# A quarter of the weights' low parts: VectorE subtraction, or negation and accumulating DMA

## The chip, the cores and the metric

The kernel runs on one core of one Trainium2 chip. The time is the device time of one execution in microseconds (us); before the change the runs shown have a median of 2719.02 us. All views of the profile come from one profiled execution.

## The reference

A trunk of two layers over 256 tokens of width 4096. All inputs are float32, and the products must keep nearly that precision.

```python
def reference(x, norm_w, w_in, q_norm, k_norm, ret_decay_fwd, ret_decay_bwd, ret_norm, w_out, final_norm):
    ...
    for l in range(DEPTH):                         # DEPTH = 2
        h = rmsnorm(x, norm_w[l])
        proj = h @ w_in[l]                         # [256, 4096] @ [4096, 11264]
        aq, ak, av, ag, rq, rk, rv, rg = jnp.split(proj, SPLIT_POINTS, axis=-1)
        ...                                        # norms of queries and keys, axial rotation
        a_out = (jax.nn.silu(ag) * gqa_attention(aq, ak, av)).astype(x.dtype)
        ...
        r = bidirectional_retention(rq, rk, rv, log_gf, log_gb).transpose(0, 2, 1, 3)
        r = rmsnorm(r, ret_norm[l]).reshape(B, S, RET_WIDTH)
        r_out = (jax.nn.silu(rg.astype(jnp.float32)) * r).astype(x.dtype)
        x = x + jnp.concatenate([a_out, r_out], axis=-1) @ w_out[l]    # [256, 4096] @ [4096, 4096]
    return rmsnorm(x, final_norm)
```

## The kernel before

Nearly all the work is two large products per layer: 256 tokens against 22 blocks of 512 columns of `w_in` and 8 such blocks of `w_out`, 30 blocks per layer and 60 in all. The contraction of 4096 is cut into 8 chunks of 512 rows. One chunk of one block is 1 MB of weights, the unit of loading: `Weights.load` issues it on SP's queue into one of three buffers `wraw` (L191, L204), after the operand's rows `full` in the first eight chunks.

TensorE multiplies in the format float32r, which keeps fewer bits than float32, so each operand is made of two parts: `hi`, the value cast to float32r, and `lo`, the rest. A product is then three matmuls (`product`, L304 to L308): `hi` with `whi`, `hi` with `wlo`, `lo` with `whi`.

The weights are split in pieces: a chunk has four row blocks of 128 rows, a piece (`WSUB = 2`) has two of them, 128 partitions x 1024 values, 512 KB. `Weights._split` makes a piece's parts: ScalarE copies `wraw` to `whi` with the cast (L219), and VectorE subtracts `whi` from `wraw` into `wlo` (L220). Both tiles have four buffers. A piece serves 2 row blocks x 2 token tiles x 3 = 12 matmuls of 128 x 128 against 512 columns, in `products`. There are 60 x 8 x 2 = 960 pieces; the very first chunk is split row block by row block, so that L219 and L220 have 962 executions.

`block` is the main loop: for each chunk and each of its two pieces the 12 matmuls, then the split of a later piece, then one step of the work beside the stream, and after the chunk the load of a later one. The split is issued under a raised priority (`AHEAD = 200`), and a scheduler orders the instructions of each engine by priority and program order. Each engine works through its own queue in order.

The work beside the stream consists of generators (`tasks`): norms, rotation, gates, transposes by 32 x 32 blocks with copies (`transposed`, L285 and L293), attention and retention with their own small products, and the residual sum. The small products go through the same `product` and stand between the large ones on TensorE.

The operand, 32 row blocks of 256 tokens in two parts, stays on the chip. Between two products of the trunk it is replaced chunk by chunk (`turn_over`): the new chunks wait in DRAM, written from POOL's queue (`put`, L254) and read back on it (`fetch`, L260), and are split by ScalarE and VectorE (`split_operand`, L237 to L244). In layer 0 the residual stream goes to DRAM on the same queue (L633). POOL otherwise computes only powers with the exponent -0.5 for the norms (L177).

At the end, the last two chunks of the last block are computed one token tile at a time, each followed by the final norm and the outputs' stores (`finish`).

Of the kernel before, what the change touches and what calls it, by code (L numbers as in the profile page):

```python
# [11 lines left out]
F32R = mybir.dt.float32r  # L12
AF = mybir.ActivationFunctionType
ALU = mybir.AluOpType
AX = mybir.AxisListType

P = 128
# [9 lines left out]
NB = 512  # L27
KT = D_MODEL // P
KG = 4
NCH = KT // KG  # L30
MT = SEQ // P
WSUB = 2
TMP = 4
ON_DVE = (0,)
# [4 lines left out]

# (kind, index, first column) of the 512-wide column blocks of w_in, in the  # L40
# order in which they are computed.
AQ, AK, AV, AG, RQ, RK, RVO, RG = 0, 2048, 2560, 3072, 5120, 6144, 7168, 9216
# [12 lines left out]

# Columns of the constants' array.
C_COS, C_SIN, C_DP, C_DN, C_END = 0, 256, 512, 1024, 1536


def constants():  # L60
    """Rotary tables and distances between positions: shapes alone."""
    rows = SEQ // GRID_W
    row = np.repeat(np.arange(rows), GRID_W).astype(np.float32)
    col = np.tile(np.arange(GRID_W), rows).astype(np.float32)
    axis = HD // 2
    inv = (10000.0 ** (-np.arange(0, axis, 2, dtype=np.float32) / np.float32(axis))).astype(np.float32)
    ar = (row[:, None] * inv[None, :]).astype(np.float64)
    ac = (col[:, None] * inv[None, :]).astype(np.float64)
    cos = np.concatenate([np.cos(ar), np.cos(ar), np.cos(ac), np.cos(ac)], axis=1)
    sin = np.concatenate([-np.sin(ar), np.sin(ar), -np.sin(ac), np.sin(ac)], axis=1)  # L70
    c = np.zeros((P, C_END), np.float32)
    for m in range(MT):
        c[:, C_COS + HD * m : C_COS + HD * (m + 1)] = cos[P * m : P * (m + 1)]
        c[:, C_SIN + HD * m : C_SIN + HD * (m + 1)] = sin[P * m : P * (m + 1)]
    j = np.arange(P)[:, None, None] + P * np.arange(MT)[None, :, None]
    d = np.arange(SEQ)[None, None, :] - j
    c[:, C_DP:C_DN] = np.maximum(d, 0).reshape(P, -1)
    c[:, C_DN:C_END] = np.maximum(-d, 0).reshape(P, -1)
    return c
# [3 lines left out]
def hybrid_encoder(  # L83
# [15 lines left out]
    nc = tc.nc  # L99
# [15 lines left out]

# [1 line left out]
    cst = t(cp, [P, C_END], "cst")  # L117
# [16 lines left out]
    def log_sigmoid():  # L134
        """lg = min(x, 0) - log1p(exp(-|x|)), log1p(u) = 2 atanh(u / (2 + u)) by its series."""
        n = DEPTH * 2 * RET_HEADS
        u, s, s2, p, a = (t(cp, [P, n], f"ls{i}") for i in range(5))
        nc.scalar.activation(a, dec, AF.Abs)
        nc.scalar.activation(u, a, AF.Exp, scale=-1.0)
        nc.vector.tensor_scalar_add(a, u, 2.0)  # L140
        nc.vector.reciprocal(a, a)
        nc.vector.tensor_mul(s, u, a)
        nc.vector.tensor_mul(s2, s, s)
        nc.vector.tensor_scalar_mul(p, s2, 1.0 / 15.0)
        for d in (13, 11, 9, 7, 5, 3):
            nc.vector.scalar_tensor_tensor(p, p, 1.0 / d, s2, op0=ALU.add, op1=ALU.mult)
        nc.vector.scalar_tensor_tensor(p, p, 1.0, s, op0=ALU.add, op1=ALU.mult)
        nc.vector.tensor_scalar(a, dec, 0.0, 0.5, op0=ALU.min, op1=ALU.mult)
        nc.vector.tensor_sub(p, a, p)
        nc.vector.tensor_scalar_mul(lg, p, 2.0)  # L150

    def halves(v, h):
        """The first or second 32 of each 64 of the last dimension: [P, ..., 2, 32]."""
        return v.rearrange("p (a b e) -> p a b e", b=2, e=HD // 4)[:, :, h, :]

    def rope_tables(kind, l):
        """Tables of cosines and signed sines, with gains and scale folded in."""
        cm = cst[:, C_COS:C_SIN].rearrange("p (m d) -> p m d", m=MT)
        sm = cst[:, C_SIN:C_DP].rearrange("p (m d) -> p m d", m=MT)
        if kind not in ("ak", "aq"):  # L160
            return cm, sm
        c = t(sp, [P, MT, HD], "C")
        s = t(sp, [P, MT, HD], "S")
        g = (kn if kind == "ak" else qn)[:, l * HD : (l + 1) * HD]
        for m in range(MT):
            nc.vector.tensor_mul(c[:, m, :], cm[:, m, :], g)
            for h in range(2):
                nc.vector.tensor_mul(halves(s[:, m, :], h), halves(sm[:, m, :], h), halves(g, 1 - h))
        if kind == "aq":
            nc.vector.tensor_scalar_mul(c, c, HD**-0.5)  # L170
            nc.vector.tensor_scalar_mul(s, s, HD**-0.5)
        return c, s

    def rsqrt(dst, ss, n, count):
        """dst = (ss / count + eps) ** -0.5 on [P, n]."""
        nc.vector.tensor_scalar(dst, ss, 1.0 / count, EPS, op0=ALU.mult, op1=ALU.add)
        nc.gpsimd.tensor_tensor(dst, dst, half[:, :n], op=ALU.pow)  # L177

# [1 line left out]
    class Weights:  # L180
        def __init__(self):
            self.todo = []
            for l in range(DEPTH):
                self.todo += [w_in[l, b, c] for b in range(N_IN) for c in range(NCH)]
                self.todo += [w_out[l, b, c] for b in range(N_OUT) for c in range(NCH)]
            self.loaded = 0
            self.raw, self.parts = [], []

        def load(self):
            if self.loaded < len(self.todo):  # L190
# [8 lines left out]
                for k in range(0, KG, step):  # L199
# [4 lines left out]
                    nc.sync.dma_start(r[:, ks, :], src[:, ks, :])  # L204
                self.raw += [(r[:, i : i + WSUB, :], step) for i in range(0, KG, WSUB)]

# [4 lines left out]
        def _split(self):  # L211
            if self.raw:
                r, step = self.raw.pop(0)
                hi = t(wp, [P, WSUB, NB], "whi", 4, F32R)
                lo = t(wp, [P, WSUB, NB], "wlo", 4, F32R)
                step = min(step, WSUB)
# [5 lines left out]

# [1 line left out]
    full = [None] * NCH  # L224
# [8 lines left out]
    def split_operand(c, gains=None):  # L233
        """hi + lo = full, its rows times gains [P, KG] if given."""
        new_operand(c)
# [14 lines left out]
    def put(c, v):  # L250
        """A finished part of the next operand waits in DRAM; the last ones stay on chip."""
        full[c] = v
# [8 lines left out]

# [1 line left out]
    tasks = []  # L263
# [15 lines left out]
    def transposed(src, room, dst):  # L279
        """dst[:, i, :] = src[:, :, i-th 128].T for i < 4; src and room are [P, MT, 512].  # L280

        Blocks of 32 x 32 are transposed in place in room, and then change places.
        """
        flat = "p m c -> p (m c)"
# [19 lines left out]
    def product(out, a, b, start, stop):  # L304
        """out += a.T @ b for operands in two parts."""
        nc.tensor.matmul(out, a[0], b[0], start=start, stop=False)  # L306
# [22 lines left out]
    def rotary(acc, L, kind, dst):  # L329
        """Queries or keys of four heads: norm, rotation, then [128, 4, 256] transposed."""  # L330
        v = evacuated(acc, L, "tmp", TMP)
# [37 lines left out]
    def gate(acc, L, dst, gain=None):  # L369
        """dst = silu of the block, times gain [P, 512] over both token tiles if given."""  # L370
        e = t(sp, [P, MT, NB], "tmp", TMP)
# [13 lines left out]
    def attention_pair(L, g, h, qT, sgT, mixT):  # L385
        """Heads h and h + 1 of group g."""
        s = [t(ps, [P, MT, SEQ], "ps") for _ in range(2)]
# [55 lines left out]
    def retention_weights(L, i):  # L443
        """(q k) * decay of two heads, [keys, queries]."""
        D = t(sp, [P, MT, 2 * SEQ], "pr", 1).rearrange("p m (a s) -> p (m a) s", a=2)
# [65 lines left out]
    def rstd_of(L, parts, n):  # L511
        """1 / rms of each token from partial sums of squares [P, MT, n]."""
        L.rstd = t(sp, [P, MT], "rstd", 2)
# [64 lines left out]
    def turn_over(c, starts, ends, l=None):  # L578
        """The operand's tiles are replaced as the last block before the change ends.

        l: the layer that begins, if one does.
        """

# [15 lines left out]
    def out_task(l, n, acc):  # L599
        """x plus the block; in the last layer times final_norm, and its sum of squares."""  # L600
        last = l == DEPTH - 1
# [38 lines left out]
    def finish(m):  # L640
        """The last block's columns of one token tile, then that tile's rows of the output."""
        n = N_OUT - 1
# [16 lines left out]

# [1 line left out]
    layers = [Layer() for _ in range(DEPTH)]  # L661
# [27 lines left out]

# [1 line left out]
    for l, L in enumerate(layers):  # L691
# [82 lines left out]
```

## Time and profile before

| What | Before |
|---|---|
| median of the runs | 2719.02 us (2718.59 to 2719.45, 2 runs) |
| profiled execution, first to last instruction | 2716.3 us |
| mean granted TensorE clock | 0.998 |
| TensorE busy | 2697.1 us (99%) |
| VectorE busy | 1768.5 us (65%) |
| ScalarE busy | 1543.6 us (57%) |
| GpSimd (POOL) busy | 55.9 us (2%) |
| DMA | 554.69 MB, mean 204 GB/s |

The profile names engines PE (matmul), PEld (weight load into TensorE), DVE (VectorE), ACT (ScalarE), POOL and SP. A line such as L220 is a line of the kernel, a tile is named by the kernel's own name, and `out<-in` says what an instruction writes and reads. A group's row gives count, busy time, mean duration in ns, and, behind the bar, the idle time of that engine just before these instructions with what ended it. A row of the waits reads: who waited, for whom, total us, times, longest. An engine that idles costs nothing while another sets the end. The matmuls are pipelined: each lasts longer than the distance to the next one.

### The profile page before, as it was taken

What the parts mean: (1) busy time and instruction counts of PE and PEld (TensorE: products, weight loads), DVE (VectorE), ACT (ScalarE), POOL (GpSimd) and SP (SyncE); (2) the same over time, 40 slices, a digit from 0 to 9 for tenths busy, and PEclk for the clock granted to TensorE, in tenths of its full rate; (3) what the DMA queues carried; (4) which work ended last, traced back from release to release, by engine and by line L of the source; (5) the groups of instructions that cost most, each with busy time, mean ns of one, the idle gap of its engine ahead of it and who ended that gap; (6) DMA issues with size and microseconds to landing.
All of it is one profiled execution on the core that took longest, in us unless ns stands there. A gap on an engine that the chain in (4) does not pass through costs nothing.

```text
span 2716.3 us, 31460 instructions
## 1 busy us (share of the span) xinstructions
PE 2697.1 (99%) x12192; PEld 2243.9 (83%) x12192; DVE 1768.5 (65%) x1995; ACT 1543.6 (57%) x2242; POOL 55.9 (2%) x78
## 2 busy tenths in 40 slices
PE   8999999999999999999999999999999999999998
PEld 7888888888888888888888888888888888888886
DVE  6677778766656675545665677787756565755544
ACT  6657667755455555545664576677555455644443
POOL 0000000000000000000000000000000000000000
PEclk9999999999999999999999999999999999999999
DMA  8654554555555565666755545555554555655654
GB/s 313 239 198 170 197 194 179 185 194 198 191 193 186 207 235 207 230 226 249 244 201 190 202 178 186 194 180 185 205 188 182 203 203 194 220 211 211 218 204 178
DMA packets 88454, 554.69 MB, mean 204 GB/s; under 512 B 9840, under 2 KB 10608, under 8 KB 26992
## 3 DMA queue, kind: packets, MB, share of 16 engines
q1 hardware_dynamic: 81968, 529.62, 54.6%
q0 software_dynamic: 6336, 23.07, 2.3%
q8 instruction: 95, 1.56, 0.2%
q14 instruction: 55, 0.45, 0.0%
HBM read 534.82 MB, written 17.83 MB: 203 GB/s over the span
## 4 chain that ended last, share of the span: by engine, by line
PE 99%; DMA 0%; issue 0%; SPq 0%; ACT 0%; DVE 0%; ACTq 0%; POOLq 0%; POOL 0%
PE acc L307 32%; PE acc L308 32%; PE acc L306 32%; PE ps L307 1%; PE ps L306 1%; PE ps L308 1%; DMA wraw<-in_w_in 0%; SPq L203 0%; SPq L204 0%; DVE wlo L220 0%; ACT whi L219 0%; ACT ps L646 0%; ACT kTh L657 0%; DVE full L644 0%; ACTq L770 0%
## 5 line engine op out<-in xcount | busy, mean ns | idle before, releaser
L220 DVE TENSOR_TENSOR wlo<-wraw,whi 128x1024 fp32r<-128x1024 f32 (+1 forms) x962 | 1165.0, 1217 | 821.0 <-ACT whi L219 818.9
L219 ACT CAST whi<-wraw 128x1024 fp32r<-128x1024 f32 (+1 forms) x962 | 1007.3, 1051 | 979.6 <-PE acc L308 945.3
L306 PE MATMUL acc<-whi,hi 128*128 128x512 f32 x3840 | 1496.2, 390 | 7.3 <-ACT whi L219 7.3
L307 PE MATMUL acc<-wlo,hi 128*128 128x512 f32 x3840 | 1495.8, 390 | 0.5 <-DVE wlo L220 0.5
L308 PE MATMUL acc<-whi,lo 128*128 128x512 f32 x3840 | 1495.7, 390 | 0.0
L306 PEld LDWEIGHTS acc<-whi,hi 128*128 128x128 f32 x3840 | 721.7, 188 | 156.0 <-ACT whi L219 7.7
L308 PEld LDWEIGHTS acc<-whi,lo 128*128 128x128 f32 x3840 | 721.5, 188 | 150.6
L307 PEld LDWEIGHTS acc<-wlo,hi 128*128 128x128 f32 x3840 | 721.7, 188 | 149.6 <-DVE wlo L220 1.4
L378 DVE RECIPROCAL tmp<-tmp 128x512 f32<-128x512 f32 x32 | 107.3, 3353 | 1.0
L293 ACT COPY tmp<-tmp 32x256 f32<-32x256 f32 x216 | 87.3, 404 | 18.5 <-DVE tmp L285 15.7
L293 ACT COPY pr<-tmp 32x256 f32<-32x256 f32 x192 | 77.5, 404 | 20.5 <-DVE tmp L285 18.1
L293 ACT COPY full<-tmp 32x256 f32<-32x256 f32 x192 | 77.5, 404 | 9.8 <-DVE tmp L285 7.3
L285 DVE STREAM_TRANSPOSE tmp<-tmp 128x1024 f32<-128x1024 f32 x42 | 52.1, 1242 | 0.9
L293 ACT COPY sg<-tmp 32x256 f32<-32x256 f32 x96 | 38.8, 404 | 12.6 <-DVE tmp L285 11.4
L401 ACT ACTIVATE pr<-ps,st 128x256 f32<-128x256 f32 x64 | 29.8, 475 | 21.2 <-DVE st L397 21.1
L316 ACT ACTIVATE tmp<-acc,rstd 128x512 f32<-128x512 f32 x36 | 24.5, 685 | 26.9 <-PE acc L308 25.6
L243 DVE SCALAR_TENSOR_TENSOR lo<-full,nw,hi 128x256 fp32r<-128x256 f32 x68 | 29.4, 479 | 9.2 <-ACT hi L242 9.2
L242 ACT ACTIVATE hi<-full,nw 128x256 fp32r<-128x256 f32 x68 | 30.1, 500 | 9.1 <-DMA full<-next_dram 3.5
L237 ACT CAST hi<-full 128x1024 fp32r<-128x1024 f32 x18 | 19.0, 1054 | 23.9 <-PE acc L307 15.8
L302 DVE TENSOR_TENSOR pTl<-pr,pTh 128x1024 fp32r<-128x1024 f32 x24 | 29.3, 1220 | 0.0
L373 ACT ACTIVATE tmp<-acc,nrstd 128x512 f32<-128x512 f32 x32 | 22.1, 691 | 10.0 <-PE acc L308 9.9
L396 DVE TENSOR_REDUCE st<-ps 128x2 f32<-128x512 f32 x32 | 21.7, 677 | 8.9 <-PE ps L308 8.9
(146 smaller groups left out, 963.7 us busy)
## 6 DMA issues: line engine op xcount, KB each, us to landing
wraw<-in_w_in SPq DMA_DIRECT2D x351, 1024.0 KB, 4.8
wraw<-in_w_out SPq DMA_DIRECT2D x128, 1024.0 KB, 4.8
next_dram<-full POOLq DMA_DIRECT2D x18, 512.0 KB, 5.1
full<-next_dram POOLq DMA_DIRECT2D x18, 512.0 KB, 4.6
tmp<-in_x SPq DMA_DIRECT2D x16, 512.0 KB, 7.1
x_dram<-tmp POOLq DMA_DIRECT2D x8, 512.0 KB, 3.9
full<-in_xT SPq DMA_DIRECT2D x7, 512.0 KB, 7.5
gain<-in_ret_norm SPq DMA_DIRECT2D x8, 256.0 KB, 3.6
```

Source lines behind the costliest of these rows:

```text
L219: nc.scalar.copy(hi[:, ks, :], r[:, ks, :])
L220: nc.vector.tensor_sub(lo[:, ks, :], r[:, ks, :], f32(hi[:, ks, :]))
L242: nc.scalar.activation(hi[c][:, k, :], full[c][:, k, :], AF.Copy, scale=g)
L243: nc.vector.scalar_tensor_tensor(lo[c][:, k, :], full[c][:, k, :], g, f32(hi[c][:, k, :]), op0=ALU.mult, op1=ALU.subtract)
L285: nc.vector.transpose(room.rearrange(flat), src.rearrange(flat))
L293: copy(to[b, :, :, i, :], fr[a, :, :, j, :])
L302: nc.vector.tensor_sub(parts[1], src, f32(parts[0]))
L306: nc.tensor.matmul(out, a[0], b[0], start=start, stop=False)
L307: nc.tensor.matmul(out, a[0], b[1], start=False, stop=False)
L308: nc.tensor.matmul(out, a[1], b[0], start=False, stop=stop)
L378: nc.vector.reciprocal(e[:, m, :], e[:, m, :])
L401: nc.scalar.activation(pr[:, m, e * SEQ : (e + 1) * SEQ], s[e][:, m, :], AF.Exp, bias=st[:, 0, i : i + 1], accum_out=st[:, 1, i : i + 1],)
```

## The change

From the ninth piece on, every fourth piece (the 12th, 16th, ..., 960th) is made in another way. ScalarE writes the negated cast of the raw weights into `wlo`; a DMA issued from POOL then reads the same weights a second time from DRAM and adds them to `wlo` where it lies, so that it holds the weights less their cast; ScalarE makes `whi` as before. VectorE has no part in such a piece. `whi` and `wlo` get five buffers in place of four, and the scratch space for the descriptors of POOL's DMAs is set to 8192 bytes per partition, where the default is 16384. Comments and docstrings are removed as well; the diff below leaves that out.

```diff
+WBUF = 5
...
     class Weights:
         def __init__(self):
...
             self.loaded = 0
+            self.n = 0
             self.raw, self.parts = [], []
...
-                self.raw += [(r[:, i : i + WSUB, :], step) for i in range(0, KG, WSUB)]
+                self.raw += [(r[:, i : i + WSUB, :], step, src[:, i : i + WSUB, :]) for i in range(0, KG, WSUB)]
...
         def _split(self):
             if self.raw:
-                r, step = self.raw.pop(0)
-                hi = t(wp, [P, WSUB, NB], "whi", 4, F32R)
-                lo = t(wp, [P, WSUB, NB], "wlo", 4, F32R)
+                r, step, src = self.raw.pop(0)
+                hi = t(wp, [P, WSUB, NB], "whi", WBUF, F32R)
+                lo = t(wp, [P, WSUB, NB], "wlo", WBUF, F32R)
+                self.n += 1
+                if self.n > 8 and self.n % 4 == 0:
+                    nc.scalar.activation(lo, r, AF.Copy, scale=-1.0)
+                    nc.gpsimd.dma_start(lo, src, accum_op=ALU.add)
+                    nc.scalar.copy(hi, r)
+                    self.parts.append((hi, lo))
+                    return
                 step = min(step, WSUB)
                 for k in range(0, WSUB, step):
                     ks = slice(k, k + step)
                     nc.scalar.copy(hi[:, ks, :], r[:, ks, :])
                     nc.vector.tensor_sub(lo[:, ks, :], r[:, ks, :], f32(hi[:, ks, :]))
                 self.parts.append((hi, lo))
...
-    nc = bacc.Bacc("TRN2", target_bir_lowering=False, num_devices=1)
+    nc = bacc.Bacc("TRN2", target_bir_lowering=False, num_devices=1, dynamic_dma_scratch_size=8192)
```

## The prediction

> **What bounds the kernel now.** I read the page first (span, busy shares, chain), then the table of stages, then the waits, then the groups and the DMA issues.
>
> ```profile
> span 2716.3 us, 31460 instructions
> PE 2697.1 (99%) x12192; PEld 2243.9 (83%) x12192; DVE 1768.5 (65%) x1995; ACT 1543.6 (57%) x2242; POOL 55.9 (2%) x78
> ...
> PE 99%; DMA 0%; issue 0%; SPq 0%; ACT 0%; DVE 0%; ACTq 0%; POOLq 0%; POOL 0%
> ```
> ```profile
> 1600.00:2000.00 400.00, 400.00 (x1852) 334.52 (x1852) 295.08 (x364) 261.73 (x421) 7.43 (x7) 1.00 0.53 190
> 2600.00:2700.00 100.00, 100.00 (x443) 82.80 (x442) 49.39 (x43) 39.38 (x43) 0.00 (x0) 1.00 0.50 181
> 2700.00:2717.00 17.00, 4.95 (x22) 3.75 (x20) 5.43 (x14) 6.57 (x12) 1.10 (x2) 0.71 0.65 247
> ```
> TensorE is busy in 2697.1 of 2716.3 us and is 99% of the chain that ended last. In the stages shown (columns: length, PE, PEld, DVE, ACT, POOL, clock, DMA share, GB/s) it is busy for the whole stage at a granted clock of 1.00. What it does not use is 2716.3 - 2697.1 = 19.2 us, of which 17.0 - 4.95 = 12.05 us are the last stage, the outputs after the last products. No change of the weights' splitting can win more than 19.2 us, 0.7%. The median of the runs, 2719.0, stands 2.7 us over the span; I carry these 2.7 us along, and make the sum against 2719.0.
>
> ```profile
> ACT whi L219 <- PE acc L308: 945.3, 607, 3.1
> DVE wlo L220 <- ACT whi L219: 818.9, 594, 3.0
> ```
> ```profile
> PE acc L306 <- ACT whi L219: 7.3, 2, 6.0
> PE acc L307 <- DVE wlo L220: 0.5, 1, 0.5
> ```
> The waits (total us, times, longest) point the same way. ScalarE waits for TensorE to give back a buffer of the weights' high part in 607 of 962 cases, VectorE waits behind ScalarE in 594, and TensorE itself waits for weights 7.8 us in all, 6.0 of them for the first piece. The split runs ahead of TensorE and is held back by it. The VectorE subtraction that the change removes is thus hidden already.
>
> **The change part by part.** The stream has 960 pieces of two row blocks (2 layers x 30 blocks x 8 chunks x 2). From piece 12 on, every fourth changes: (960 - 8) / 4 = 238.
>
> ```profile
> L220 DVE TENSOR_TENSOR wlo<-wraw,whi 128x1024 fp32r<-128x1024 f32 (+1 forms) x962 | 1165.0, 1217 | 821.0 <-ACT whi L219 818.9
> L219 ACT CAST whi<-wraw 128x1024 fp32r<-128x1024 f32 (+1 forms) x962 | 1007.3, 1051 | 979.6 <-PE acc L308 945.3
> L242 ACT ACTIVATE hi<-full,nw 128x256 fp32r<-128x256 f32 x68 | 30.1, 500 | 9.1 <-DMA full<-next_dram 3.5
> ```
> *Removed:* 238 subtractions x 1.217 = 290 us of VectorE, 1768 to 1479 us. VectorE is on no part of the chain: worth 0.
>
> *Added on ScalarE:* 238 negations. Their form is not in the trace; the CAST of the same size takes 1.05 us, and four of the scaled copies of a quarter of the size 4 x 0.50 = 2.0. I take the CAST's 1.05 (same size): 250 us, 1544 to 1794 us, 66% of the span; at 2.0 it would be 74%. In the stage 1600 to 2000, with 261.7 of 400 us, 37 us come on top: 75%. The cover is ScalarE's waiting above; gone, it would cost up to these 250 us.
>
> *Added on the DMA queues:* 238 accumulating DMAs of 512 KB, issued from POOL.
>
> ```profile
> q1 hardware_dynamic: 81968, 529.62, 54.6%
> q0 software_dynamic: 6336, 23.07, 2.3%
> ...
> wraw<-in_w_in SPq DMA_DIRECT2D x351, 1024.0 KB, 4.8
> ...
> next_dram<-full POOLq DMA_DIRECT2D x18, 512.0 KB, 5.1
> full<-next_dram POOLq DMA_DIRECT2D x18, 512.0 KB, 4.6
> x_dram<-tmp POOLq DMA_DIRECT2D x8, 512.0 KB, 3.9
> ```
> ```profile
> L260 POOL DMA_DIRECT2D full<-next_dram x18: 527/538/582, 927.2 to 2335.4; - x18
> ...
> DMA to landing us min/median/max: 3.5/4.6/7.2
> ```
> An accumulation into SBUF is not in the trace. The nearest rows are the 44 plain transfers of the same 512 KB on the same queue (18 + 18 + 8): they hold the 16 engines for 2.3% x 2716.3 / 44 = 1.42 us each, and land 4.6 us (loads) or 5.1 us (stores) after issue. Lower end: an accumulation costs what a load costs, 1.42 us of the engines and 4.6 us to landing. Upper end by rows: it reads SBUF as a store does and loads as a load does, one behind the other: 4.6 + 5.1 = 9.7 us. I take twice the engine time, since it reads two operands for one write: 2.84 us, landing 4.6 + 1.42 = 6.0 us.
>
> The Trainium skill (Collectives: The Full Stack, "The bandwidth ceiling: the fold count and why AG ≠ RS ≠ AR") says that an adding DMA is slower than a copying one because it needs two source reads, not because of the add, so that its rate is about half. By that rule the engine time is 2.84 us, as taken; without it the bounds 1.42 and up stand as they are. No row here shows an adding DMA.
>
> *How long the landing may take.* TensorE's pace is the clock:
>
> ```profile
> 1000.11 0.39 PE L306 MATMUL acc<-whi,hi 128*128 128x512 f32 x1
> ...
> 1002.83 0.39 PE L306 MATMUL acc<-whi,hi 128*128 128x512 f32 x1
> ```
> These two starts are 12 matmuls apart, one piece: 2.72 us, 0.227 us per matmul. In the instructions of the built program, five buffers in place of four let a negation start once the piece five places earlier is consumed, and the first matmul that reads the summed low part stands 51 matmuls later in 168 of the 238 cases, 56 to 75 later in 64, 50 in 5, and 33 for the last piece. Fifty matmuls take 11.34 us; less 0.39 - 0.23 = 0.16 for the end of the releasing matmul, 1.05 for the negation and 0.1 for hand-overs, 10.0 us are left for the landing. Against 6.0 that is 4.0 us spare, against 9.7 it is 0.3.
>
> *What eats the spare time.* The longest landing of a plain load is 7.2 - 4.6 = 2.6 us over the median, and ScalarE works in order, so a negation can stand behind other work:
>
> ```profile
> 1144.35 1.05 ACT L219 CAST whi<-wraw 128x1024 fp32r<-128x1024 f32 x1
> 1145.42 2.48 ACT L293 COPY full<-tmp 32x256 f32<-32x256 f32 x6
> 1147.93 1.05 ACT L219 CAST whi<-wraw 128x1024 fp32r<-128x1024 f32 x1
> ```
> A string of six copies holds ScalarE for 2.48 us. Both together: 6.0 + 2.6 + 2.5 = 11.1, 1.1 us too late. ScalarE was busy at the release in (962 - 607) / 962 = 37% of the pieces, and the longest of 18 landings is 1 in 18: 0.37 / 18 x 238 = 5 cases, 5 us at most. I take 2 us. At the upper end (9.7), ScalarE's 37% alone make 88 cases late by about 1 us: 92 us. The last piece has 32 x 0.227 - 1.31 = 5.9 us: 0.1 us late, 3.8 at the upper end; I take 1 us.
>
> *Moved:* on POOL each accumulation stands among the 44 transfers and the small powers of the norms. Nothing that stands ahead of one on POOL depends, in the built order, on a later matmul than its own negation does; behind it wait the powers, which VectorE needs. An issue holds POOL 0.54 us (row above), every 10.9 us. Worth 0, with the rival below if POOL blocks. The smaller descriptor ring, 8192 for the default 16384 bytes, has no row; with one accumulation per 10.9 us and 6.0 to landing hardly more than one is in flight: 0, at the worst a POOL transfer that waits for the one before it.
>
> *Engine time of the DMAs.* Four pieces are 4 x 2.72 = 10.9 us. The two queues above hold the engines 56.9% of it, 6.2 us; with 2.84 it is 9.0 us, 83%. Bytes read grow by 238 x 0.524 = 125 MB, to 250 GB/s on average, and the first slice of the page already moves 313.
>
> ```profile
> GB/s 313 239 198 170 197 194 179 185 194 198 191 193 186 207 235 207 230 226 249 244 201 190 202 178 186 194 180 185 205 188 182 203 203 194 220 211 211 218 204 178
> ```
> *Sum:* 2719.0 + 0 (VectorE) + 0 (ScalarE, hidden) + 2 (late landings) + 1 (last piece) = 2722 us. With the low ends 2719; with the high ends 2719 + 92 + 4 = 2815.
>
> **The rivals.**
> *A, the accumulation overloads the DMA engines* (slower). If it holds them k times as long as a plain load, a group of four pieces needs 6.2 + 1.42 k; above k = 3.3 this is more than 10.9 us and TensorE starves at the rate of the DMAs. At k = 4 it is 11.9 us, 1.0 too long: 238 x 1.0 = 240 us, 2959; each further k adds 338 us. For it: no row shows how an engine does read, add and write, and the engines are over half used. Against it: nothing but the two-reads argument.
> *B, landings at the top of the bounds* (slower): a negation that finds ScalarE busy then stalls TensorE, the 2815 us worked out above. For it: weights' transfers and accumulations share the engines, and the plain loads already spread to 7.2. Against it: 9.7 supposes no overlap of the two reads.
> *C, POOL in order* (slower or within): the 18 fetches wait for a buffer to come free, and an accumulation behind one waits as well.
>
> ```profile
> POOL full L260 <- DVE lo L238: 111.6, 6, 42.3
> ```
> The 42.3 is POOL's idle time since its previous work, not a hold-up by itself. At 1 us for each of POOL's 78 operations it is 78 us, 2797.
> *D, the change does what it says and a gain appears:* at most 19.2 us, 2700, still within 2%.
>
> **How the numbers follow.** The forecast has 0.62 (its own range 2714 to 2750); A 0.22; B 0.10; C 0.05; D 0.01. Some of B and C stays under 2% (2773; 2% is about what a measurement of this kernel can tell from no change): 0.03. So within 2%: 0.62 + 0.03 + 0.01 = 0.66 or so; slower by more: 0.33; faster by more: 0.01, since TensorE's idle time does not allow it. The time is that of the forecast, 2722. The range goes from 2708 (half of the possible gain and a little) to 2960, which takes in B, C and A up to k = 4, and leaves out the heavier half of A, 0.12, and some 0.02 below.
>
> **What would show it.** Right: the new row of the DMA issues lands near 6 us, q0 grows by about 238 x 2.84 / 2716 = 25% to 27%, VectorE falls to about 1480 us and ScalarE rises to about 1794, and TensorE's waits for the accumulation stay under 10 us in all. Wrong: q0 above 45% and weights landing far over 4.8 us (A), landings over 10 us with a wait of TensorE in most groups (B), or waits of accumulations behind other POOL work (C). A negation far from 1.05 us would break ScalarE's term.

## The result and the profile after

The changed kernel takes 2754.48 us (2754.42 to 2754.53, two runs) against 2719.02: 1.0134 times the time before, interval 1.0117 to 1.0152. That is 35 us slower, within the 2% and within the range that the prediction gave, on the side of its forecast but some twelve times as far from the time before as its 2722. The prediction took about 2% for what a measurement of this kernel can tell from no change; the interval shows that a loss of 1.3% is clear.

The page after, rows in the order of the first fences of the prediction:

```profile
span 2752.7 us, 32073 instructions
PE 2710.4 (98%) x12192; PEld 2242.7 (81%) x12192; DVE 1491.3 (54%) x1757; ACT 1765.2 (64%) x2480; POOL 264.1 (10%) x316
...
q1 hardware_dynamic: 81968, 529.62, 51.9%
q0 software_dynamic: 40608, 147.87, 31.0%
...
PE 68%; issue 19%; DMA 8%; DVE 2%; ACT 1%; POOL 1%; SPq 0%; POOLq 0%; ACTq 0%
...
wraw<-in_w_in SPq DMA_DIRECT2D x351, 1024.0 KB, 7.1
wraw<-in_w_out SPq DMA_DIRECT2D x128, 1024.0 KB, 7.2
wlo<-in_w_in POOLq DMA_DIRECT2D x174, 512.0 KB, 8.3
wlo<-in_w_out POOLq DMA_DIRECT2D x64, 512.0 KB, 8.4
```

The span is 36.4 us longer. The chain is no longer TensorE alone: accumulations (the `wlo<-in_w_...` DMAs, 238 of them) hold 7 to 8% of it. ("issue" is time in which an engine waited for nothing that the profile shows.) VectorE has become 277 us lighter, ScalarE 222 us heavier. Loads of weights now take 7.1 us to land where they took 4.8.

The waits after (who waited, for whom, total us, times, longest):

```profile
POOL wlo L221 <- ACT wlo L220: 2012.4, 221, 34.1
DVE wlo L229 <- ACT whi L228: 896.5, 467, 7.1
ACT whi L228 <- PE acc L317: 527.5, 349, 4.4
...
PEld acc L316 <- DMA wlo<-in_w_in: 25.4, 31, 3.3
```
```profile
PE acc L316 <- DMA wlo<-in_w_in: 14.6, 15, 2.9
PE acc L315 <- ACT whi L228: 7.8, 2, 5.8
PE acc L316 <- DMA wlo<-in_w_out: 7.6, 8, 2.2
PE acc L316 <- DVE wlo L229: 0.5, 1, 0.5
```

TensorE has one new wait, 14.6 + 7.6 = 22.2 us for accumulations, in 23 places. That is nearly all of its additional idle time: span less busy is 42.3 us after, 19.2 before, 23.1 more. The other 13 us are busy time: 2710.4 - 2697.1. I added up the distances between the starts of neighbouring matmuls as far as they exceed 227 ns: 8.3 us before (6.3 of them at the start), 44.8 after, 36.5 more, the whole loss. Behind each stall the next matmul starts some 335 in place of 227 ns later, and after the two longest the clock drops. So the loss is stalls of TensorE and what follows directly on each.

One stall, step by step (start, duration, engine):

```profile
1343.45 1.30 ACT L251 ACTIVATE hi<-full,nw 128x256 fp32r<-128x256 f32 x3
...
1344.78 0.40 ACT L302 COPY full<-tmp 32x256 f32<-32x256 f32 x1
1345.21 1.06 ACT L220 ACTIVATE wlo<-wraw 128x1024 fp32r<-128x1024 f32 x1
...
1346.29 0.53 POOL L269 DMA_DIRECT2D full<-next_dram  x1 [8.46 <-DVE lo L252]
1346.81 0.93 POOL L221 DMA_DIRECT2D wlo<-in_w_out  x1
...
1347.23 7.03 SPq L206 DMA_DIRECT2D wraw<-in_w_out  x2
```
```profile
1346.81 10.30 DMA wlo<-in_w_out
1357.11 0.04 issue
1357.16 0.50 PE acc L316
```

ScalarE starts the negation late, behind other work (its buffer had been free for about 1.5 us). POOL first issues a fetch and then the accumulation. 0.4 us later SP issues loads of weights. The accumulation lands 10.3 us after issue, and TensorE starts 0.04 us after that.

### The profile page after: what moved, and what is told of

The parts are those of the page before. It is cut to its first block, busy times and chain, and to the rows that moved or that the text cites. A ratio compares the mean times of both kernels' runs of the same rounds, so it can differ in the third digit from the quotient of the medians.

```text
span 2752.7 us, 32073 instructions
## 1 busy us (share of the span) xinstructions
PE 2710.4 (98%) x12192; PEld 2242.7 (81%) x12192; DVE 1491.3 (54%) x1757; ACT 1765.2 (64%) x2480; POOL 264.1 (10%) x316
## 3 DMA queue, kind: packets, MB, share of 16 engines
q1 hardware_dynamic: 81968, 529.62, 51.9%
## 4 chain that ended last, share of the span: by engine, by line
PE 68%; issue 19%; DMA 8%; DVE 2%; ACT 1%; POOL 1%; SPq 0%; POOLq 0%; ACTq 0%
PE acc L316 22%; PE acc L317 22%; PE acc L315 22%; DMA wlo<-in_w_in 4%; DMA wlo<-in_w_out 3%; DVE wlo L229 1%; POOL wlo L221 1%; PE ps L316 1%; PE ps L315 1%; PE ps L317 1%; DVE tmp L632 0%; DMA wraw<-in_w_in 0%; DVE pTl L311 0%; ACT whi L228 0%; ACT full L302 0%
## 5 line engine op out<-in xcount | busy, mean ns | idle before, releaser
L316 PE MATMUL acc<-wlo,hi 128*128 128x512 f32 x3840 | 1501.9, 391 | 23.1 <-DMA wlo<-in_w_in 14.6
L229 DVE TENSOR_TENSOR wlo<-wraw,whi 128x1024 fp32r<-128x1024 f32 (+1 forms) x724 | 877.6, 1216 | 898.0 <-ACT whi L228 896.5
L228 ACT CAST whi<-wraw 128x1024 fp32r<-128x1024 f32 (+1 forms) x724 | 757.3, 1050 | 629.8 <-PE acc L317 527.5
L220 ACT ACTIVATE wlo<-wraw 128x1024 fp32r<-128x1024 f32 x238 | 252.3, 1060 | 213.2 <-PE acc L316 212.3
L221 POOL DMA_DIRECT2D wlo<-in_w_in x174 | 151.0, 868 | 1613.4 <-ACT wlo L220 1468.5
L222 ACT CAST whi<-wraw 128x1024 fp32r<-128x1024 f32 x238 | 245.6, 1032 | 15.9 <-PE acc L317 15.9
L221 POOL DMA_DIRECT2D wlo<-in_w_out x64 | 55.6, 868 | 544.7 <-ACT wlo L220 543.9
L386 DVE TENSOR_SCALAR tmp<-tmp 128x512 f32<-128x512 f32 x32 | 13.6, 424 | 55.9 <-ACT tmp L382 55.9
```

The source lines that it names most:

```text
L220: nc.scalar.activation(lo, r, AF.Copy, scale=-1.0)
L221: nc.gpsimd.dma_start(lo, src, accum_op=ALU.add)
L222: nc.scalar.copy(hi, r)
L228: nc.scalar.copy(hi[:, ks, :], r[:, ks, :])
L229: nc.vector.tensor_sub(lo[:, ks, :], r[:, ks, :], f32(hi[:, ks, :]))
L316: nc.tensor.matmul(out, a[0], b[1], start=False, stop=False)
```

## The experiments

All times below are medians, each with its ratio to the kernel before on the same chip, where that took 2717.0 to 2718.3 us. A few words for the theories: L is that accumulations land later than TensorE needs them.

**What of the change costs.** Three kernels keep parts of it. The first has five buffers and the smaller descriptor ring alone:

```diff
-                if self.n > 8 and self.n % 4 == 0:
+                if False:
```

> Five buffers and the smaller descriptor ring alone; every low part is subtracted on VectorE. Theory L (late landings: the accumulations arrive after TensorE needs them): 2719 us, within 3, since no accumulation is left. Rival S (the other order of instructions that five buffers and the ring bring): a good part of the 35 us stays, over 2735.

2717.9 us, ratio 1.0001 (0.9992 to 1.0011). Buffers and ring cost nothing, and with one more buffer nothing is won either.

The second keeps the negations on ScalarE and adds on VectorE:

```diff
-                    nc.gpsimd.dma_start(lo, src, accum_op=ALU.add)
+                    nc.vector.tensor_add(lo, r, f32(lo))
```

> ScalarE's negation stays in every fourth piece, and VectorE adds the weights to it where the DMA did. Theory L: 2719 us, within 4; TensorE's waits for weights stay near the 8 us of before. Rival N (the 250 us of negations delay ScalarE's other casts and with them TensorE): 2735 to 2755, with TensorE waiting behind ScalarE or VectorE.

2722.0 us, 1.0016 (1.0007 to 1.0025). The negations alone cost about 4 us, 2.3 of them a new wait of the attention's products, none a wait for weights:

```profile
PE acc L315 <- ACT whi L228: 6.8, 2, 6.0
PE ps L316 <- DVE pTl L311: 2.3, 6, 0.4
PE acc L316 <- DVE wlo L229: 0.5, 1, 0.5
```

The third keeps negations, issues and bytes, but copies in place of adding:

```diff
-                    nc.gpsimd.dma_start(lo, src, accum_op=ALU.add)
+                    nc.gpsimd.dma_start(lo, src)
```

> The same negations and the same DMAs from POOL, but plain, not accumulating, so that the low part of every fourth piece is the whole weights. Theory L with the cost in read-add-write: packets of 4096 B fall from about 327 to about 160 ns, the median landing from 8.4 to about 6.5 us, and the time to 2720 to 2730, with stalls only where ScalarE starts the negation over 2.5 us late. Rival T (it is the second transfer as such, its issue on POOL and its 125 MB, that costs): landings stay over 8 us and the time at 2745 to 2755.

2721.0 us, 1.0015 (1.0006 to 1.0025). The second transfer as such is not the cost. Its rows of `wlo`, and then those of the changed kernel:

```profile
L221 POOL DMA_DIRECT2D wlo<-in_w_in x174: 527/527/689, 33.9 to 2343.8; - x174
...
DMA to landing us min/median/max: 3.8/5.0/10.5
```
```profile
L221 POOL DMA_DIRECT2D wlo<-in_w_in x174: 852/863/1020, 34.5 to 2376.1; - x174
...
DMA to landing us min/median/max: 5.5/8.4/12.8
```

Adding in place of copying takes POOL 0.86 us to issue in place of 0.53, and the median landing goes from 5.0 to 8.4 us. The shortest landing, 5.5 and 3.8 us, is in both kernels that of the last piece, which meets no load of weights: alone, adding costs 1.6 us more, beside the loads 3.4. In the records of the packets 4096 bytes most often last 327 ns with the addition and 174 ns in the plain copies of the same weights. The longest plain landing is 10.5 us, but such are too few to matter. So some 32 of the 35 us (1.0134 less 1.0015) hang on adding in place of copying.

**Time to the landing.** The same change with one buffer fewer of both parts:

```diff
-WBUF = 5
+WBUF = 4
```

> Four buffers of both parts in place of five, 12 matmuls or 2.72 us less time for the landing. Theory L: moving each accumulation's spare time in the profile of the change down by 2.72 us leaves 202 of 237 late, by 345 us in all: 3060 us, or 2980 and up if the stalls spread the transfers. Rival R (the stalls come from a few rare meetings, such as strings of ScalarE copies, and the common case has time enough): 26 stalls grow by 2.7 us each, about 2825.

3080.6 us, 1.1333 (1.1315 to 1.1351). The forecast 3060 came from taking 2.72 us from the spare time of each accumulation one by one; it is close, and the rival's 2825 is out. The landings themselves have hardly changed (median 8.1 us). TensorE waits for accumulations in 203 places:

```profile
PE acc L316 <- DMA wlo<-in_w_in: 177.6, 142, 4.1
PE acc L316 <- DMA wlo<-in_w_out: 83.6, 61, 3.5
```

The other way, a sixth buffer for the low parts:

```diff
-                lo = t(wp, [P, WSUB, NB], "wlo", WBUF, F32R)
+                lo = t(wp, [P, WSUB, NB], "wlo", WBUF + 1, F32R)
...
-    nc = bacc.Bacc("TRN2", target_bir_lowering=False, num_devices=1, dynamic_dma_scratch_size=8192)
+    nc = bacc.Bacc("TRN2", target_bir_lowering=False, num_devices=1, dynamic_dma_scratch_size=4096)
```

> The low parts get six buffers, the high parts keep five, and the descriptor ring gives up the room for it (4096 bytes). In the built order the first matmul that reads an accumulated piece moves from 51 to 62 matmuls behind its release, 2.5 us more time. Theory L (landings later than about 10 us after the negation's start, late by at most 3.0 us in the profile of the change): nearly all 26 stalls vanish, 2719 to 2724 us, VectorE still 290 us lighter. Rival B (the DMA engines as such are short of time): landings grow and the time stays over 2740.

2730.4 us, 1.0045 (1.0028 to 1.0061). Two thirds of the loss are gone, not nearly all of it, and the expected 2719 to 2724 is missed. 22.2 us of waiting have become 8.7 in 7 places:

```profile
PE acc L316 <- DMA wlo<-in_w_in: 7.7, 6, 2.4
PE acc L316 <- DMA wlo<-in_w_out: 1.0, 1, 1.0
```
```profile
DMA to landing us min/median/max: 5.4/6.6/12.1
```

The sixth buffer changed two things at once. It gives more time to the landing, and the landings themselves became shorter, 6.6 us at the median in place of 8.4. In the change a load of weights is issued within 1 us of the accumulation, before or behind it, in 233 of 238 cases; here in 59, which land in 8.8 us (median), while the other 179 land in 5.8. This run does not tell how much of the 24 us is due to which.

Most of the waiting that is left lies in the first 100 us, where the inputs are loaded as well, and where the operand is replaced (near 990, 1350 and 1375 us); there ScalarE starts a negation as late as 6.9 us after the piece five places before was consumed.

**When the accumulation meets the weights.** With every fourth piece, the last of a chunk, the same piece frees the raw buffer; in the trace the next load of weights is issued 0.67 us behind the accumulation in most cases. So accumulation and load run in step, as it is called below. The first piece of a chunk in its place:

```diff
-                if self.n > 8 and self.n % 4 == 0:
+                if self.n > 8 and self.n % 4 == 1:
```

> The accumulated piece is the first of every second chunk in place of the last (13th, 17th, ... 957th). In the profile of the change a load of 1 MB of weights is issued 0.67 us behind nearly every accumulation, because the same piece frees the raw buffer, and the two share the engines. Theory C (this collision makes the landing 8.4 us long): out of step the landing falls to 6 to 7 us and the time to 2720 to 2730. Rival: the read-add-write alone is the length, the landing stays at 8 us or more, and the time at 2745 to 2760.

2759.1 us, 1.0163 (1.0145 to 1.0180). Half of it came as expected: the median landing fell from 8.4 to 7.0 us. The time did not follow, because the late ones got later:

```profile
DMA to landing us min/median/max: 5.2/7.0/13.0
```
```profile
PE acc L316 <- DMA wlo<-in_w_out: 17.0, 7, 3.6
PE acc L316 <- DMA wlo<-in_w_in: 13.2, 10, 2.7
```

The execution that was profiled took 2769.0 us, the three others 2757.6 to 2759.8, so its waits are somewhat over the usual. In at least 10 of its 18 longer stalls another transfer of POOL, mostly a store of the next operand, was in flight when the accumulation was. With these 44 transfers on SP's queue (first piece of a chunk as above):

```diff
-            nc.gpsimd.dma_start(next_dram[c], v.rearrange("p k s -> p (k s)"))
+            nc.sync.dma_start(next_dram[c], v.rearrange("p k s -> p (k s)"))
...
-            nc.gpsimd.dma_start(full[c].rearrange("p k s -> p (k s)"), next_dram[c])
+            nc.sync.dma_start(full[c].rearrange("p k s -> p (k s)"), next_dram[c])
...
-        nc.gpsimd.dma_start(x2_dram[n].rearrange("p (m n) -> p m n", m=MT), res)
+        nc.sync.dma_start(x2_dram[n].rearrange("p (m n) -> p m n", m=MT), res)
```

> As e4_first_half (first piece of every second chunk), and the other 44 transfers of POOL go out on SP's queue, so that POOL's queue holds accumulations alone. In the profile of e4_first_half, 10 of the 18 stalls have another POOL transfer in flight beside the accumulation, landings 10 to 13 us. Theory Q (the accumulation queues behind them on the one software queue): landings over 10 us get rare, and the time falls from 2759 to 2725 to 2740. Rival: they meet on the 16 engines whatever the queue, the landings stay and the time at 2750 or more.

2747.2 us, 1.0109 (1.0094 to 1.0124): 12 us better, between theory and rival. The longest landing fell from 13.0 to 11.1 us, TensorE's wait from 30.2 to 13.7 us. So these transfers on POOL's queue account for a part of the loss. Whether it is the shared queue, or that SP issues them at other times, the run does not tell; that the rest comes from meetings on the DMA engines is not shown. Then the sixth buffer of the low parts on top of this kernel:

> The first piece of every second chunk, POOL's other transfers on SP's queue (e9_fh_sp), and six buffers of the low parts. Theory L: the late landings of e9_fh_sp, at most 3.1 us late, find 2.5 us more: 2719 to 2726. If late landings were not what is left in e9_fh_sp, it stays at 2740 or more.

2743.4 us, 1.0096 (1.0079 to 1.0113): a miss. The extra buffer lets the negation start earlier, and the median landing went back from 6.5 to 8.3 us:

```profile
L221 POOL DMA_DIRECT2D wlo<-in_w_in x174: 862/865/1023, 27.3 to 2357.2; - x174
...
DMA to landing us min/median/max: 5.5/8.3/12.1
```

The earlier start puts the accumulation back in step with the loads of weights: one is issued within 1 us of it in 213 of 238 cases, against 22 in the kernel without this buffer. With the landings longer, the buffer gained only some 4 us here, against 24 on top of the change, where it made them shorter. That the step alone makes this difference is argued, not tested.

**ScalarE in order.** In the trace of the change 16 of 26 stalls over 0.2 us (counted from start to start of the matmuls, less 0.227 us), 17.9 of 26.7 us, follow a negation that ScalarE began more than 1.3 us after its buffer was free. The transposes' copies are most of what stands ahead, so they go to VectorE:

```diff
-ON_DVE = (0,)
+ON_DVE = (0, 1, 2, 3)
```

> The change, with the 696 block copies of the transposes (0.40 us each on ScalarE, 0.28 on VectorE) moved from ScalarE to VectorE, which the change has freed by 290 us. In the profile of the change 16 of the 26 stalls, 17.9 of their 26.7 us, begin with a negation that starts over 1.3 us late behind such copies. Theory O (ScalarE in order makes these late): they vanish, 2730 to 2738 us. Rival: the landings alone decide, or the copies on VectorE hold back POOL's descriptors, and the time stays at 2745 or more.

2764.4 us, 1.0174 (1.0159 to 1.0189): slower, against the expectation. Negations start earlier now (ScalarE's share fell from 64 to 54%), and stalls in the attention's stage shrink from about 1.3 to 0.75 us. In the output products a new wait took over. POOL holds the store of the next operand until the last copy is made, and the accumulation stands behind it. First the changed kernel, then this one:

```profile
1166.80 0.55 POOL L263 DMA_DIRECT2D next_dram<-full  x1 [8.24 <-ACT full L302]
1167.89 0.89 POOL L221 DMA_DIRECT2D wlo<-in_w_out  x1 [0.53 <-ACT wlo L220]
```
```profile
1168.80 0.55 POOL L263 DMA_DIRECT2D next_dram<-full  x1 [9.05 <-DVE full L302]
1169.34 0.93 POOL L221 DMA_DIRECT2D wlo<-in_w_out  x1
```

In the first the accumulation waits for its negation (0.53 us); in the second the negation was long done, 2.1 us before POOL came to the accumulation. That the copies hold back POOL's descriptors, the other part of the rival, does not show: the median issue lasts 0.86 us as before. With the sixth buffer this wait has room:

> Six buffers of the low parts (e5_lo6) and the copies on VectorE. Theories L and O together: hardly a stall is left but those in the first 100 us, 2719 to 2725. If e5_lo6's remaining 12 us come from the DMA engines alone, it stays near 2730.

2727.2 us, 1.0038 (1.0023 to 1.0053), against 1.0045 with the sixth buffer alone: the same within their intervals, and just over the expected 2719 to 2725. No version here beats the kernel before.

**Twice as many accumulations.**

```diff
-                if self.n > 8 and self.n % 4 == 0:
+                if self.n > 8 and self.n % 2 == 0:
```

> Every second piece is accumulated, 476 in place of 238. By the engines' time (plain transfers 1490 us, an accumulation 3.3 us): 1490 + 476 x 3.3 = 3060 us, over the 2719 of TensorE, so that the DMA engines become the bound: 3060 to 3300. Rival: each accumulation costs what it costs now, 35 us per 238: 2790.

2887.9 us, 1.0627 (1.0610 to 1.0643), between both and under the expected 3060 to 3300. The stages from 400 to 2400 us, first of this kernel, then of the change (length, PE, PEld, DVE, ACT, POOL, clock, DMA share, GB/s):

```profile
400.00:2400.00 2000.00, 1924.01 (x8540) 1567.62 (x8539) 868.06 (x1082) 1405.42 (x1932) 332.85 (x392) 0.99 0.98 277
```
```profile
400.00:2400.00 2000.00, 1985.68 (x8993) 1646.52 (x8992) 1111.16 (x1295) 1307.53 (x1840) 198.44 (x240) 1.00 0.83 245
```

The DMA engines are nearly full here, 0.98, where the change left them at 0.83. What TensorE waits for is still the single accumulation:

```profile
PE acc L316 <- DMA wlo<-in_w_in: 81.2, 75, 5.7
PE acc L316 <- DMA wlo<-in_w_out: 29.6, 29, 3.4
```

The median landing is 9.7 us, and TensorE's waits for the parts that the plain loads feed have not grown (7.9 us behind ScalarE, 7.8 in the change). So full engines and later landings come together, and the run does not show that the engines' rate by itself sets the time. My 3060 was too high because 3.3 us is no fixed cost of an accumulation: by this kernel's page the software queue holds the engines 49.7% of 2892.2 us; less 62 us for the plain transfers that is 2.89 us for each of the 476.

## Why the prediction was right, and where it was not

The forecast, no change beyond 2%, came true, but with luck: of its own five signs of being right only VectorE and ScalarE did. The landing (8.4 us for 6), the software queue (31.0% for 25 to 27) and TensorE's waits (22.2 us for under 10) did not, and with 2.72 us less time for the landing (four buffers) the loss was 13%.

**TensorE is the bound, and relieving VectorE is worth nothing:** right. The kernel with plain copies, whose VectorE is as light as in the change (1490.5 us), is at 1.0015, and no variant that takes work from VectorE is faster than before.

**The work on each engine:** right within 2%. The negation took 1.06 us (1.05 taken), VectorE came to 1491 us (1479), ScalarE to 1765 (1794).

**Engine time of an accumulation:** 31.0% of 2752.7 us less 62, over 238, is 3.32 us, k = 2.3, where 2.84 (k = 2) was taken. Both queues together hold 83%, as forecast, only because the share of the plain loads fell from 54.6 to 51.9%. The plain copy in the same place takes 20.7% of 2718.6 us less 62, over 238: 2.10 us, so that the base of 1.42 was too low here as well, and the mean factor is 1.58. The Trainium skill's rule of two source reads (Collectives: The Full Stack, "The bandwidth ceiling: the fold count and why AG ≠ RS ≠ AR"), which the page gives for ReduceScatter against AllGather, makes a factor of about two; the most frequent packets are near it, 327 ns to 174, a factor of 1.88.

**The landing is the step that failed:** 6.0 us taken, 8.3 to 8.4 measured, in the upper half of the bounds 4.6 to 9.7. The term added the doubled engine time to the landing of transfers that start at other times than the loads of weights. What it left out is that the same piece starts the accumulation and frees the raw buffer for the next load, 0.67 us later, so that they nearly always run against each other. The plain copy in the same place lands in 5.0 us, the accumulation out of step in 7.0, in step in 8.4. For the one accumulation that runs alone, the last, the doubled engine time fits: 3.8 us of the plain copy and 1.42 are 5.2, measured 5.5. What the term put at nothing is the meeting with the loads.

**The spare time of 10.0 us:** right but for hand-overs, which take 0.3 us in place of 0.1, and the most useful number of the working: where the negation starts at once, a landing of 10.19 us gave a stall of 0.45, so 9.7 us were left. With 2.72 us taken from it the time came out at 3081 where it gave 3060.

**Late landings, 2 us taken:** the mis-sized term of the sum. The stalls are 22.2 us of waiting, 36.5 with what follows. With 8.4 in place of 6.0 the spare time is 1.6 us, and a ScalarE string of 2.5 us, a neighbour on POOL's queue or a crowded stretch is each enough by itself; the forecast had allowed only for the coincidence of two. The upper end of the same term, 92 us, holds.

**The last piece, 1 us:** its accumulation landed 5.5 us after issue, within the 5.9 us it had; no stall there.

**The rivals:** B had the mechanism, landings near the top and a ScalarE that is busy, and its 2815 was too far. A was not reached (k = 2.3 against 3.3); the kernel with twice as many accumulations comes near it, with the engines at 0.98. C is a minor part: 12 us between the two kernels that differ in POOL's other transfers (with the other piece of a chunk), and the new wait when the copies moved. D did not appear.

## What to carry to other kernels

When one engine has nothing left to give, taking work from another cannot win, and each new producer in front of it can only add waits; a prediction should then price the wait and not the work saved. Work out the time between a buffer's release and its next use, and set against it the landing as it will be beside the transfers that start with it; a landing in the trace before, of transfers that start at other times, is too short. Landings decide by their late cases: a shorter median gained nothing while the longest grew. One buffer more gained 24 us where it also took the transfers out of step, and 4 us where it put them into step: after a change of timing, look again at what starts together.

## What the runs showed of the hardware

After a pause of TensorE its granted clock can be half for a while. After the stall above, 2.20 us idle, its matmuls go from 0.23 to 0.43 us apart within 1.4 us, and the granted clock of the stretch falls to 0.72:

```profile
1356.00:1362.00 6.00, 4.84 (x14) 3.87 (x15) 1.10 (x3) 2.13 (x4) 1.41 (x2) 0.72 0.99 316
```
```profile
1357.16 0.50 PE L316 MATMUL acc<-wlo,hi 128*128 128x512 f32 x1 [2.20 <-DMA wlo<-in_w_out]
...
1359.00 0.63 PE L316 MATMUL acc<-wlo,hi 128*128 128x512 f32 x1
1359.42 0.63 PE L317 MATMUL acc<-whi,lo 128*128 128x512 f32 x1
```

The record of the clock has 3.41 us at 0.5 there and the same after the 2.9 us wait at 68 us, and none after pauses of 1.9 us or less from start to start in this run (the first matmuls and the end of the program apart). By this each such record costs about 1.7 us, half of its length (an estimate). In the kernel that accumulates the first piece of a chunk, with all of POOL's transfers on POOL, one pause of 3.9 us had no such record, so the clock can fall after a pause and need not.
